# x's normalised combinations made in the first projections, and one PSUM pool for all stages

## The chip, the core and the metric

The kernel runs on one core of a Trainium2 chip. The metric is device time of one execution in microseconds (us), taken as the median of several runs; smaller is better. One execution was also recorded by the hardware profiler, and all rows below come from that one.

## What is computed

One decoder layer on x of 512 tokens by 2048 channels, in fp32. h = RMSNorm(x) goes through one wide projection w_in (2048 rows) that yields the queries, keys and values of three token mixers (A: sliding window, B: forgetting attention, C: cross attention into a memory), a SiLU path z for each of them, and 3 x 2048 columns of merge-gate logits:

```
proj = rms_norm(x, norm_gain) @ w_in
ua = (ya * silu(za)) @ w_branch_a        # ub, uc in the same way
g  = sigmoid(gate_logits).reshape(b, s, 3, D)
y  = g[:, :, 0]*ua + g[:, :, 1]*ub + g[:, :, 2]*uc
out = x + y @ w_out
```

## The kernel before, in words

Every fp32 operand of a matmul is split into a high and a low part (fp32r), and a product is three matmuls: high by high, low by high, high by low. ACT makes the high part (a copy), DVE the low part (a subtraction). 

The program is one order written out by hand: instructions of PE, DVE, ACT and POOL stand in the order in which the Python code emits them. A counter `clock` advances by half a slot for every three matmuls of the main stream (`tick`, line 127), and `later(dt, f)` emits f that many slots afterwards, so that side work is sprinkled between matmuls. The DMAs of SP are not in that order: they are put in order by the building layer, by when their inputs and buffers come free; SP then works through them one after another.

**Main stream** (class `Stream`, line 209). Chunks of up to 512 columns, each of 8 units; a unit takes 2 tiles of 128 rows of w_in and is 24 matmuls. In order: qB0, kB0, vB0 (the first chunk group), qB1, kB1, vB1 (the second), qA0, qA1, kvA, z0, mem, qC, z1, z2, z3. The x operands are the tiles `ah`, `al` (x times norm_gain, high and low; line 63); `rstdb` is the row of 1/rms of all tokens. Unit i asks for the split of unit i+1's weights and for the load of unit i+2's (`run`, line 244): `wa` is the raw tile, `wb` and `wc` the high and low part. A chunk has four PSUM banks from `psum_pj` (tag pj, 4 buffers). The attention heads run beside the stream with banks of the tags T and S (2 buffers each). These 8 banks are one PSUM pool, `ps`.

**z chunks** (`evac_z`, line 909): DVE multiplies each of the four banks by `rstdb` (L926), multiplies the mixer's output y by it (L929), ACT takes the sigmoid, and DVE multiplies again (L932); y then goes to HBM.

**Gates and output** (classes `Late`, `Product`, `Blocks`, lines 1007 to 1212) use a Strassen-Winograd scheme: x is cut into pairs u of two 128-row tiles and two halves of 256 tokens, four blocks a, b, c, d of 128x256; seven products of sums of blocks take the place of eight. A block of gates has 8 units of four products (P1, P5, P6, P4; x operands a, s1, s2, d in `xhx`, `xlx`) and then 8 units of three (P2, P7, P3; operands s3, c, s4 in `yhx`, `ylx`). The banks are tags b0 to b3 with 2 buffers each in a second PSUM pool `pl`, which is opened after `ps` is closed (lines 1470 and 1471).

**The step between them** (`plan_x`, line 1215, and `combine_both`). While z2 and z3 run, each pair u of x is loaded again from HBM (512 KB), DVE normalises it (two 128x512 operations, L1223), makes s1 = b+d, s2 = s1-a, s3 = a-b, s4 = c-s2 (four of 128x256, L1000 and L1003), and the high and low parts are made: 4 blocks into the place of `ah[u]`, `al[u]` as z3 has done with them, 3 blocks into new tiles. `late.step` places the loads, sums and splits of the first gate units in the same stretch.

Of the kernel before, what the change touches and what calls it, by code (L numbers as in the profile page):

```python
# [19 lines left out]
P = 128  # L20
# [23 lines left out]
def tile_hybrid_block(ctx, tc, xT, x, memT, mem, ng, mng, w_in, b_forget, gqa, gka, sinks, gqb, gkb, gqc, gkc,  # L44
# [158 lines left out]

    def psum_pj(name):
        return ps.tile([P, 512], F32, tag="pj", bufs=4, name=name)

    class Stream:
# [37 lines left out]
        def run(self, i):  # L245
# [264 lines left out]
    def tbank(name):  # L510
        return ps.tile([P, 512], F32, tag="T", bufs=2, name=name)

    def sbank(name):
        return ps.tile([P, 512], F32, tag="S", bufs=2, name=name)

    def avbank(name):
        return ps.tile([P, 512], F32, tag="T", bufs=2, name=name)

# [485 lines left out]

    def combine_both(u, xs, s, name, dx):

        bl = blocks(xs)
        a, b, c, d = (bl[:, i, :] for i in range(4))
        add(s[:, 0, :], b, d)
        sub(s[:, 1, :], s[:, 0, :], a)  # L1010
        sub(b, a, b)

        def first():
            h, l = x_tiles(u, name)
            parts(h[:, 0:4:3, :], l[:, 0:4:3, :], bl[:, 0:4:3, :])
            parts(h[:, 1:3, :], l[:, 1:3, :], s, 1)
            later(1, second)

        def second():
            sub(d, c, s[:, 1, :])  # L1020
            parts(*y_tiles(u, name), bl[:, 1:4, :])
        later(dx, first)

# [39 lines left out]
    class Product:  # L1063
# [62 lines left out]
    TAGS = ("b0", "b1", "b2", "b3")  # L1126

# [87 lines left out]
    def plan_x(left):  # L1215


        def one(u, xs, s, free_at):
            fetch_x(xs, u, xT)

            def norm():
                for k in range(2):
                    ve.scalar_tensor_tensor(out=xs[:, k, :], in0=xs[:, k, :], scalar=ngt[:, 2 * u + k:2 * u + k + 1],  # L1223
                                            in1=rstdb, op0=ALU.mult, op1=ALU.mult)
            later(3.5, norm)
            later(4, lambda: combine_both(u, xs, s, "x", max(0.5, free_at - clock[0])))

        def low(u, at):
            t = raw_tile()
            one(u, t[:, 0:2, :], t[:, 2, :].rearrange("p (k n) -> p k n", k=2), at)  # L1230
# [56 lines left out]
    class Branch:  # L1287
# [27 lines left out]
        def run(self):  # L1315
# [87 lines left out]
    def outputs(cpair, tags):  # L1403
# [62 lines left out]
    with tc.tile_pool(name="gp", bufs=1) as pool:  # L1466
        gp.append(pool)
        plan_x(4 * (n_p5 - k))
        run(k, n_p5)
        psp.__exit__(None, None, None)  # L1470
        with tc.tile_pool(name="pl", bufs=2, space=PSUM) as pool:
            gp.append(pool)
            late.run(0, n_gates - 8)
            plan_ys()
            late.run(n_gates - 8, len(late.units))
            flush()
        manual.__exit__(None, None, None)
# [37 lines left out]
```

## Time and profile before

| | us |
|---|---|
| median of 3 runs | 1547.23 (1546.73 to 1547.9) |
| the profiled execution, its own time | 1548.03 |
| its span, first to last instruction | 1546.3 |
| PE busy in the span | 1496.5 (97%) |
| DVE busy | 1085.1 (70%) |
| ACT busy | 723.3 (47%) |
| POOL busy | 269.3 (17%) |

Busy times are sums of instruction times. An engine executes its instructions in order, and one that waits holds back all behind it. PE is the engine that nearly always works, so the places where it does not are where time can go or come from: the view of waits names what ended each of PE's pauses, the timeline shows its instructions one by one (start, duration, and in brackets the pause before it and what ended it), and the windows view gives busy time and the granted clock of TensorE (1.00 is 2.4 GHz, 0.50 is 1.2 GHz) for a stretch. A matmul's row is longer than the step to the next one, since matmuls overlap; what counts is from start to start.

### The profile page before, as it was taken

To read this page: it belongs to the slowest core of one execution; us is meant where nothing else is said; L and a number is where in the kernel's file an instruction comes from. 1 tells how busy PE (TensorE), PEld (TensorE's weight loads), DVE (VectorE), ACT (ScalarE), POOL (GpSimd) and SP (SyncE) were. 2 spreads that over 40 slices of the span, in tenths; PEclk is the share of its full clock that TensorE was granted. 3 is DMA by queue.
4 is the path that set the end of the run, shared out by engine and by line. 5 is a ranking of instruction groups with operands and counts; after the bars stand their busy time and mean duration, and the time that the engine had idled before them with its cause. 6 is when DMAs were issued, how large, how long until landed. Compare 5 with 4: busy or idle time off the path is not lost.

```text
span 1546.3 us, 20410 instructions
## 1 busy us (share of the span) xinstructions
PE 1496.5 (97%) x7233; PEld 1278.0 (83%) x7233; DVE 1085.1 (70%) x1810; ACT 723.3 (47%) x1206; POOL 269.3 (17%) x295
## 2 busy tenths in 40 slices
PE   8999999999999999997999999999999999999998
PEld 7999999998877888875787878787878788877876
DVE  7554664664587755489877777878787656589986
ACT  5434654664477644444435353444445422236432
POOL 3322660661324432100000000000000101110000
PEclk9999999999999999998999999999999999999999
DMA  6443333232254222553667676757676866567583
GB/s 200 135 119 94 89 86 92 76 89 82 89 170 139 81 82 69 163 177 125 229 191 243 192 232 192 235 187 240 194 233 204 286 203 194 171 227 256 191 294 138
DMA packets 118222, 258.53 MB, mean 167 GB/s; under 512 B 13020, under 2 KB 47964, under 8 KB 118120
## 3 DMA queue, kind: packets, MB, share of 16 engines
q1 hardware_dynamic: 113944, 242.54, 49.8%
q10 hardware_dynamic: 4176, 14.69, 2.9%
q8 instruction: 57, 0.93, 0.2%
q14 instruction: 45, 0.37, 0.1%
HBM read 233.04 MB, written 24.14 MB: 166 GB/s over the span
## 4 chain that ended last, share of the span: by engine, by line
PE 71%; DVE 14%; ACT 6%; DMA 4%; issue 3%; SPq 1%; ACTq 0%; POOL 0%; DVEq 0%; POOLq 0%
PE P L1058 27%; PE z L282 8%; PE kB L282 4%; PE vB L282 4%; PE qA L282 4%; PE uB L1058 3%; PE kvA L282 3%; PE uA L1058 3%; PE qC L282 3%; DVE rawl L1003 2%; PE qB L282 2%; DVE R L1000 2%; PE uC L1058 2%; DVE wd L1101 2%; ACT R L1250 2%
## 5 line engine op out<-in xcount | busy, mean ns | idle before, releaser
L1098 ACT CAST wa<-rawl 128x1024 fp32r<-128x1024 f32 x128 | 134.7, 1053 | 257.8 <-PE P L1058 131.0
L196 DVE TENSOR_TENSOR wc<-wa,wb 128x512 fp32r<-128x512 f32 (+2 forms) x254 | 162.1, 667 | 106.4 <-ACT wb L193 105.8
L1003 DVE TENSOR_TENSOR rawl<-rawl 128x512 f32<-128x512 f32 (+1 forms) x265 | 180.6, 682 | 24.8 <-DMA rawl<-in_w_in_dram 14.9
L193 ACT CAST wb<-wa 128x512 fp32r<-128x512 f32 (+2 forms) x254 | 131.3, 565 | 133.1 <-PE z L282 42.2
L1101 DVE TENSOR_TENSOR wc<-rawl,wa 128x1024 fp32r<-128x1024 f32 x128 | 156.3, 1221 | 51.4 <-ACT wa L1098 51.2
L1347 POOL TENSOR_TENSOR y<-y,gA 128x512 f32<-128x512 f32 x16 | 24.7, 1554 | 717.5 <-DMA rawl<-in_w_b_dram 596.9
L1098 ACT CAST wb<-rawl 128x512 fp32r<-128x512 f32 (+1 forms) x128 | 107.1, 837 | 68.9 <-PE P L1058 54.0
L1101 DVE TENSOR_TENSOR wd<-rawl,wb 128x512 fp32r<-128x512 f32 (+1 forms) x128 | 121.8, 951 | 13.8 <-ACT wb L1098 13.7
L282 PE MATMUL z<-ah,wb 128*128 128x512 f32 x256 | 102.5, 400 | 0.8 <-DVE zA L926 0.8
L282 PE MATMUL z<-ah,wc 128*128 128x512 f32 x256 | 100.1, 391 | 0.0
L282 PE MATMUL z<-al,wb 128*128 128x512 f32 x256 | 99.8, 390 | 0.0
L1058 PE MATMUL P<-wa,xhx 128*128 128x512 f32 x192 | 75.8, 395 | 11.2 <-DVE zC L926 11.2
L1058 PE MATMUL P<-wd,xhx 128*128 128x512 f32 x192 | 76.3, 398 | 4.7 <-DVE wd L1101 4.7
L1058 PE MATMUL P<-wb,xhx 128*128 128x512 f32 x192 | 76.0, 396 | 2.0 <-ACT wb L1098 1.3
L1058 PE MATMUL P<-wc,xhx 128*128 128x512 f32 x192 | 75.6, 394 | 0.7 <-DVE wc L1101 0.7
L1058 PE MATMUL P<-wa,xlx 128*128 128x512 f32 x192 | 75.7, 394 | 0.0
L1058 PE MATMUL P<-wb,xlx 128*128 128x512 f32 x192 | 75.0, 390 | 0.0
L1058 PE MATMUL P<-wa,yhx 128*128 128x512 f32 x192 | 74.7, 389 | 0.0
L1058 PE MATMUL P<-wa,ylx 128*128 128x512 f32 x192 | 74.7, 389 | 0.0
L1058 PE MATMUL P<-wc,yhx 128*128 128x512 f32 x192 | 74.7, 389 | 0.0
L1000 DVE TENSOR_TENSOR R<-P,R 128x512 f32<-128x512 f32 x88 | 56.1, 684 | 20.0 <-PE P L1058 19.5
L572 POOL TENSOR_SCALAR pB<-pB,denB 128x128 f32<-128x128 f32 (+3 forms) x48 | 55.3, 1152 | 49.3 <-DVE denB L571 36.5
(385 smaller groups left out, 4022.6 us busy)
## 6 DMA issues: line engine op xcount, KB each, us to landing
rawl<-in_w_in_dram SPq DMA_DIRECT2D x144, 512.0 KB, 4.2
rawl<-in_w_out_dram SPq DMA_DIRECT2D x48, 512.0 KB, 4.6
wa<-in_w_in_dram SPq DMA_DIRECT2D x63, 384.0 KB, 3.3
wa<-in_w_in_dram SPq DMA_DIRECT2D x64, 256.0 KB, 3.0
rawl<-in_w_in_dram SPq DMA_DIRECT2D x48, 256.0 KB, 4.1
gates<-R ACTq DMA_DIRECT2D x24, 512.0 KB, 8.0
wa<-in_w_in_dram SPq DMA_DIRECT2D x16, 512.0 KB, 3.7
wa<-in_w_mem_dram SPq DMA_DIRECT2D x16, 512.0 KB, 3.3
```

Of the source, the lines that this page charges most:

```text
L193: ac.copy(hi[:, :n], raw[:, i, :n])
L196: ve.tensor_sub(lo[:, :n], raw[:, i, :n], f32(hi[:, :n]))
L282: pe.matmul(pb, a, m, start=b in fresh, stop=last and not todo[b])
L572: po.tensor_scalar(p, p, den[:, 4 + i:5 + i], None, op0=ALU.mult)
L1000: ve.tensor_tensor(out, a, b, op=ALU.add)
L1003: ve.tensor_tensor(out, a, b, op=ALU.subtract)
L1058: pe.matmul(*args, **kw)
L1098: ac.copy(hi[:, :k, :], src)
L1101: return lambda: ve.tensor_tensor(lo[:, :k, :], src, f32(hi[:, :k, :]), op=ALU.subtract)
L1250: ac.activation(r, r, AF.Sigmoid)
L1347: po.tensor_tensor(y, y, g, op=ALU.add)
```

## The change

`plan_sums` is new. During the first two chunk groups it loads each pair of x as four pieces of 128x256, normalises them, makes the four sums in place, and stores two sets in HBM: a, s1, s2, d (`x_alpha`, 512 KB a pair) and s3, c, s4 (`x_beta`, 384 KB). The tiles are the places ys3 to ys6, which are empty at that time. `plan_x` then only loads these sets and splits them (one high and one low operation for each set). The loads of the first three gate units are asked for 4 to 6 slots earlier, and for the last z chunk the two y multiplications and the sigmoid are emitted later. There is one PSUM pool of four tags with 2 buffers each for the whole program: T becomes b0, S becomes b1, a chunk's banks 0 and 1 are b2, 2 and 3 are b3. The rotation of tags among gates, branches and outputs is turned by two, so that the first gate products P1, P5, P6, P4 are in b0, b1, b2, b3.

```diff
-    psp = tc.tile_pool(name="ps", bufs=1, space=PSUM)
-    ps = psp.__enter__()
+    ps = ctx.enter_context(tc.tile_pool(name="ps", bufs=2, space=PSUM))
+    TAGS = ("b0", "b1", "b2", "b3")
...
+    xad = nc.dram_tensor("x_alpha", (D // 2, 1024), F32, kind="Internal").ap()
+    xbd = nc.dram_tensor("x_beta", (D // 2, 768), F32, kind="Internal").ap()
...
-    def psum_pj(name):
-        return ps.tile([P, 512], F32, tag="pj", bufs=4, name=name)
+    def bank(i, name):
+        return ps.tile([P, 512], F32, tag=TAGS[i], name=name)
...
-                    banks[b] = psum_pj(f"{name}_{b}")
+                    banks[b] = bank(2 + b // 2, f"{name}_{b}")
...
-            later(0.5, lambda: ve.tensor_tensor(y, y, z, op=ALU.mult))
+            later(1.5 + 1.5 * b if c == 3 else 0.5, lambda: ve.tensor_tensor(y, y, z, op=ALU.mult))
...
-                later(1, lambda: [ac.activation(z, z, AF.Sigmoid) for z, _ in mul])
-                later(4, mul[0][1])
-                later(5, mul[1][1])
+                tail = c == 3
+                later(8 if tail else 1, lambda: [ac.activation(z, z, AF.Sigmoid) for z, _ in mul])
+                later(13 if tail else 4, mul[0][1])
+                later(19 if tail else 5, mul[1][1])
...
-    def combine_both(u, xs, s, name, dx):
...
+    def plan_sums(t0):
+        def one(u, n):
+            xa, xb = (place(i, f"x{i}s{u}").rearrange("p k (t n) -> p (k t) n", t=2) for i in (n, n + 1))
+            a, s1, s2, d = (xa[:, i, :] for i in range(4))
+            s3, c, s4, b = (xb[:, i, :] for i in range(4))
+            rows = [slice((2 * u + k) * P, (2 * u + k + 1) * P) for k in range(2)]
+            halves = [slice(0, 256), slice(256, 512)]
+            for dst, k, h in ((a, 0, 0), (b, 0, 1), (c, 1, 0), (d, 1, 1)):
+                sy.dma_start(out=dst, in_=xT[rows[k], halves[h]])
+            def norm(dst, k, h):
+                ve.scalar_tensor_tensor(out=dst, in0=dst, scalar=ngt[:, 2 * u + k:2 * u + k + 1],
+                                        in1=rstdb[:, halves[h]], op0=ALU.mult, op1=ALU.mult)
+            def store():
+                r = slice(u * P, (u + 1) * P)
+                sy.dma_start(out=xad[r, :].rearrange("p (k n) -> p k n", n=256), in_=xa)
+                sy.dma_start(out=xbd[r, :].rearrange("p (k n) -> p k n", n=256), in_=xb[:, 0:3, :])
+            steps = [lambda: (norm(a, 0, 0), norm(b, 0, 1)), lambda: (norm(c, 1, 0), norm(d, 1, 1)),
+                     lambda: (add(s1, b, d), sub(s2, s1, a)), lambda: (sub(s3, a, b), sub(s4, c, s2)), store]
+            for i, f in enumerate(steps):
+                later(5.5 + 1.5 * i, f)
+        for u in range(NP):
+            at_slot(t0 + (0, 9, 18, 27, 44, 72, 100, 128)[u], lambda u=u: one(u, 3 + 2 * (u % 2)))
...
-                        self.banks[m, t] = gp[1].tile([P, 512], F32, tag=self.tags[n], name=f"{m}_{wcnt[0]}_{t}")
+                        self.banks[m, t] = bank(self.tags[n], f"{m}_{wcnt[0]}_{t}")
...
     def plan_x(left):
-        def one(u, xs, s, free_at):
...
+        def alpha(u):
+            xs = place(2 + u % 2, f"xa{u}").rearrange("p k (t n) -> p (k t) n", t=2)
+            sy.dma_start(out=xs, in_=xad[u * P:(u + 1) * P, :].rearrange("p (k n) -> p k n", n=256))
+            later(5, lambda: parts(*x_tiles(u, "x"), xs, 1))
+        def beta(u):
+            if u % 2 == 0:
+                beta.t = raw_tile()
+            xs = beta.t[:, 2 * (u % 2):2 * (u % 2) + 2, :].rearrange("p k (t n) -> p (k t) n", t=2)[:, 0:3, :]
+            sy.dma_start(out=xs, in_=xbd[u * P:(u + 1) * P, :].rearrange("p (k n) -> p k n", n=256))
+            later(5, lambda: parts(*y_tiles(u, "x"), xs, 1))
         t0 = left - 32
...
+            later(max(0, t0 - 16 + 2.5 * u), lambda u=u: beta(u))
+            later(t0 - 0.5 + 4 * u, lambda u=u: alpha(u))
-        for dt, what, i in ((17, "load", 0), (20, "load", 1), (23, "load", 2), (26, "sums", 0), (28, "early", 0), (29, "sums", 1)):
+        for dt, what, i in ((11, "load", 0), (15, "load", 1), (19, "load", 2), (21, "sums", 0), (23, "sums", 1), (25, "sums", 2),
+                            (28, "early", 0)):
...
-        turn = 2 + 3 * (len(late.units) // (2 * NP))
-        tags = [TAGS[(turn + n) % 4] for n in range(4)]
+        turn = 3 * (len(late.units) // (2 * NP))
+        tags = [(turn + n) % 4 for n in range(4)]
...
     later(20, x_rows)
+    plan_sums(clock[0] + 26)
     run(8, n_p1)
...
-        psp.__exit__(None, None, None)
-        with tc.tile_pool(name="pl", bufs=2, space=PSUM) as pool:
-            gp.append(pool)
```

How the order moves. The rows name line, operation, output<-inputs and shape; a number behind a name tells buffers apart. PE's and POOL's orders stay as they were.

DVE at the end of z3, from the evacuation of its first bank (z_0) to past that of its last (z_3). `wc`, `wd` from a `rawl` are low parts of gate weights, `xlx`, `ylx` low parts of x. Before:

```order
L926 TENSOR_TENSOR zC_7132<-z_0_6780,rstdb 128x512
L1003 TENSOR_TENSOR rawl_7011<-rawl_7011 128x512 x3
L989 TENSOR_TENSOR xlx_7138<-xs_7073,xhx_7137 128x2x256
L926 TENSOR_TENSOR zC_7132<-z_1_6781,rstdb 128x512
L989 TENSOR_TENSOR xlx_7138<-ss_7074,xhx_7137 128x512
L1003 TENSOR_TENSOR xs_7073<-xs_7073,ss_7074 128x256
L929 TENSOR_TENSOR ysC_6212<-ysC_6212,zC_7132 128x1024
L1101 TENSOR_TENSOR wc_7114<-rawl_6979,wa_7113 128x1024
L989 TENSOR_TENSOR ylx_7152<-xs_7073,yhx_7151 128x768
L926 TENSOR_TENSOR zC_7168<-z_2_6782,rstdb 128x512
L926 TENSOR_TENSOR zC_7168<-z_3_6783,rstdb 128x512
L1223 SCALAR_TENSOR_TENSOR xs_7123<-xs_7123,ngt,rstdb 128x512 x2
```

and now:

```order
L992 TENSOR_TENSOR xlx_7186<-xa_7128,xhx_7185 128x1024
L928 TENSOR_TENSOR zC_7231<-z_0_6917,rstdb 128x512
L1112 TENSOR_TENSOR wc_7218<-rawl_7038,wa_7217 128x1024
L992 TENSOR_TENSOR xlx_7226<-xa_7173,xhx_7225 128x1024
L928 TENSOR_TENSOR zC_7231<-z_1_6918,rstdb 128x512
L928 TENSOR_TENSOR zC_7253<-z_2_6919,rstdb 128x512
L1112 TENSOR_TENSOR wd_7240<-rawl_7038,wb_7239 128x1024
L928 TENSOR_TENSOR zC_7253<-z_3_6920,rstdb 128x512
L1112 TENSOR_TENSOR wc_7260<-rawl_7080,wa_7259 128x1024
L931 TENSOR_TENSOR ysC_6340<-ysC_6340,zC_7231 128x1024
```

The norms and sums of the last pairs and the triple weight sums are gone from between the evacuations, and the y multiplication stands behind the second weight part.

DVE in the second and third unit of vB0 (`wc` is a stream weight's low part, `t_kB`, `nr_kB` the norm of the keys). Before:

```order
L401 TENSOR_SCALAR nr_kB_836<-nr_kB_836 128x6
L196 TENSOR_TENSOR wc_859<-wa_798,wb_858 128x384
L407 TENSOR_TENSOR t_kB_808<-t_kB_808,nr_kB_822 128x384
L400 TENSOR_REDUCE nr_kB_850<-sq_kB_856 128x6
L401 TENSOR_SCALAR nr_kB_850<-nr_kB_850 128x6
L196 TENSOR_TENSOR wc_859<-wa_798,wb_858 128x384
L407 TENSOR_TENSOR t_kB_808<-t_kB_808,nr_kB_836 128x384
L407 TENSOR_TENSOR t_kB_808<-t_kB_808,nr_kB_850 128x384
```

and now:

```order
L198 TENSOR_TENSOR wc_867<-wa_804,wb_866 128x384
L1021 SCALAR_TENSOR_TENSOR x4s_782<-x4s_782,ngt,rstdb 128x256
L1021 SCALAR_TENSOR_TENSOR x3s_781<-x3s_781,ngt,rstdb 128x256
L409 TENSOR_TENSOR t_kB_814<-t_kB_814,nr_kB_828 128x384
L402 TENSOR_REDUCE nr_kB_858<-sq_kB_864 128x6
L403 TENSOR_SCALAR nr_kB_858<-nr_kB_858 128x6
L198 TENSOR_TENSOR wc_867<-wa_804,wb_866 128x384
L409 TENSOR_TENSOR t_kB_814<-t_kB_814,nr_kB_842 128x384
L1003 TENSOR_TENSOR x3s_781<-x4s_782,x3s_781 128x256
L1006 TENSOR_TENSOR x3s_781<-x3s_781 128x256
L409 TENSOR_TENSOR t_kB_814<-t_kB_814,nr_kB_858 128x384
```

Two of the four pairs of 128x256 operations on x's first pair (`x3s`, `x4s`) stand among the same rows; the first pair of norms stands a few rows ahead of them, the last two subtractions follow.

SP in vB0 (`wa` are the stream's raw weights, `c_rows` and `cb` belong to attention B). Before:

```order
L183 DMA wa_908<-in_w_in_dram 128x2x384
L183 DMA wa_955<-in_w_in_dram 128x2x384
L183 DMA wa_995<-in_w_in_dram 128x2x384
L183 DMA wa_1040<-in_w_in_dram 128x2x384
L494 DMA c_rows<-f_cum 12x512
L183 DMA wa_1072<-in_w_in_dram 128x2x384
L770 DMA cb_1223<-c_rows 128x512 x2
```

and now:

```order
L185 DMA wa_928<-in_w_in_dram 128x2x384
L1026 DMA x_alpha<-x3s_781 128x1024
L1027 DMA x_beta<-x4s_782 128x768
L185 DMA wa_977<-in_w_in_dram 128x2x384
L1018 DMA x3s_1018<-in_xT_dram 128x256 x2
L1018 DMA x4s_1019<-in_xT_dram 128x256 x2
L185 DMA wa_1029<-in_w_in_dram 128x2x384
L1026 DMA x_alpha<-x5s_905 128x1024
L1027 DMA x_beta<-x6s_906 128x768
L185 DMA wa_1078<-in_w_in_dram 128x2x384
L496 DMA c_rows<-f_cum 12x512
```

The weights' loads have stores of one pair of x and loads of the next but one ahead of them, and a load into `x3s` has to wait until the store from it has landed.

## Rows read from the trace of the kernel before

**Rows 1.** The page, from its first line, part 1 and part 2 (40 equal slices of the span; PEclk is the granted clock in tenths).
```profile
span 1546.3 us, 20410 instructions
...
PE 1496.5 (97%) x7233; PEld 1278.0 (83%) x7233; DVE 1085.1 (70%) x1810; ACT 723.3 (47%) x1206; POOL 269.3 (17%) x295
...
PEclk9999999999999999998999999999999999999999
```

**Rows 2.** The view of waits, engine PE, whole span: who waited for whom, us in total, times, longest.
```profile
PE P L1058 <- DVE zC L926: 11.2, 1, 11.2
```

**Rows 3.** The windows view: stretch, its length, busy time (and instructions) of PE, of PE's weight loads, DVE, ACT, POOL, then granted clock, DMA share, GB/s.
```profile
122.00:249.00 127.00, 126.04 (x761) 123.39 (x760) 73.85 (x185) 71.37 (x160) 61.79 (x80) 1.00 0.32 89
...
642.00:742.00 100.00, 87.21 (x370) 70.43 (x368) 81.27 (x128) 40.42 (x59) 0.00 (x0) 0.93 0.53 173
...
724.00:726.00 2.00, 1.86 (x5) 1.51 (x6) 2.00 (x3) 0.32 (x1) 0.00 (x0) 0.50 0.70 249
...
730.00:735.00 5.00, 5.00 (x24) 4.12 (x23) 4.51 (x7) 1.61 (x3) 0.00 (x0) 1.00 0.34 87
```

**Rows 4.** PE's timeline from the start of z3 to the second gate unit: start, duration, line, what, and in brackets the pause before it and what ended that.
```profile
671.19 0.50 PE L282 MATMUL z<-ah,wb 128*128 128x512 f32 x1 [0.75 <-DVE zA L926]
...
712.59 0.39 PE L282 MATMUL z<-ah,wc 128*128 128x512 f32 x1
724.14 0.77 PE L1058 MATMUL P<-wa,xhx 128*128 128x512 f32 x1 [11.16 <-DVE zC L926]
...
729.25 0.40 PE L1058 MATMUL P<-wb,xhx 128*128 128x512 f32 x1
...
732.24 0.39 PE L1058 MATMUL P<-wa,xlx 128*128 128x512 f32 x1
732.47 0.39 PE L1058 MATMUL P<-wc,xhx 128*128 128x512 f32 x1
...
738.76 0.50 PE L1058 MATMUL P<-wc,xhx 128*128 128x512 f32 x1 [0.70 <-DVE wc L1101]
...
743.09 0.50 PE L1058 MATMUL P<-wd,xhx 128*128 128x512 f32 x1 [1.27 <-DVE wd L1101]
```

**Rows 5.** DVE's timeline around the end of z3, columns as in the group before.
```profile
714.78 0.68 DVE L926 TENSOR_TENSOR zC<-z,rstdb 128x512 f32<-128x512 f32 x1
...
718.03 0.68 DVE L926 TENSOR_TENSOR zC<-z,rstdb 128x512 f32<-128x512 f32 x1
...
720.71 1.22 DVE L1101 TENSOR_TENSOR wc<-rawl,wa 128x1024 fp32r<-128x1024 f32 x1
...
722.71 1.28 DVE L926 TENSOR_TENSOR zC<-z,rstdb 128x512 f32<-128x512 f32 x2
```

**Rows 6.** Groups of DVE instructions by line and shape from 640 to 761 us: count, busy us, mean ns, idle before them.
```profile
L1101 DVE TENSOR_TENSOR wc<-rawl,wa 128x1024 fp32r<-128x1024 f32 x8 | 9.7, 1217 | 0.0
...
L1223 DVE SCALAR_TENSOR_TENSOR xs<-xs,ngt,rstdb 128x512 f32<-128x512 f32 x10 | 7.0, 745 | 0.0
L989 DVE TENSOR_TENSOR ylx<-xs,yhx 128x768 fp32r<-128x768 f32 x5 | 4.8, 955 | 2.7 <-ACT yhx L988 2.7
...
L989 DVE TENSOR_TENSOR xlx<-rawl,xhx 128x512 fp32r<-128x512 f32 x6 | 3.9, 683 | 0.0
L1003 DVE TENSOR_TENSOR rawl<-rawl 128x256 f32<-128x256 f32 x9 | 3.5, 421 | 0.1
```

**Rows 7.** DVE's timeline in vB0 and at the end of vB1.
```profile
90.19 0.56 DVE L196 TENSOR_TENSOR wc<-wa,wb 128x384 fp32r<-128x384 f32 x1 [0.99 <-ACT wb L193]
...
91.80 0.55 DVE L196 TENSOR_TENSOR wc<-wa,wb 128x384 fp32r<-128x384 f32 x1
...
93.57 0.56 DVE L407 TENSOR_TENSOR t_kB<-t_kB,nr_kB 128x384 f32<-128x384 f32 x1 [0.74 <-POOL nr_kB L363]
...
94.31 0.56 DVE L196 TENSOR_TENSOR wc<-wa,wb 128x384 fp32r<-128x384 f32 x1
...
248.81 0.62 DVE L444 SCALAR_TENSOR_TENSOR V_vB<-vB,rstds,V_vB 128x384 fp32r<-128x384 f32 x1 [0.42 <-ACT V_vB L443]
```

**Rows 8.** PE's timeline: the first uses of three of those weight parts, and the first matmul of qA0 into the bank that the last row above sets free.
```profile
93.71 0.33 PE L282 MATMUL vB<-wc,ah 128*128 128x384 f32 x1
...
95.79 0.33 PE L282 MATMUL vB<-wc,ah 128*128 128x384 f32 x1
...
126.42 0.34 PE L282 MATMUL qB<-wc,ah 128*128 128x384 f32 x1
...
249.56 0.36 PE L282 MATMUL qA<-wb,ah 128*128 128x384 f32 x1
```

**Rows 9.** The view of line L196 from 122 to 249 us: duration in ns (least, median, most), first and last start, shape.
```profile
L196 DVE TENSOR_TENSOR wc<-wa,wb x48: 537/555/965, 122.9 to 246.2; 128x384 fp32r<-128x384 f32 x48
```

**Rows 10.** POOL's longest common group by shape from 50 to 340 us: count, busy us, mean ns, idle before.
```profile
L572 POOL TENSOR_SCALAR pB<-pB,denB 128x512 f32<-128x512 f32 x10 | 17.1, 1710 | 17.3 <-DVE denB L571 17.3
```

**Rows 11.** SP's timeline: a run of nine issues of weights; the first, at 115.17, fetches those of the unit that PE starts at 126.16.
```profile
115.17 35.88 SPq L183 DMA_DIRECT2D wa<-in_w_in_dram  x9
```

**Rows 12.** The view of DMA issues: count, KB each, median us from issue to landing.
```profile
wa<-in_w_in_dram SPq DMA_DIRECT2D x63, 384.0 KB, 3.3
...
gates<-R ACTq DMA_DIRECT2D x24, 512.0 KB, 8.0
...
ys_B<-ysB SPq DMA_DIRECT2D x3, 512.0 KB, 4.7
```

More of the change, by code (lines that the diff above doesn't have):

```diff
@@ L510, in tbank @@
     def tbank(name):
-        return ps.tile([P, 512], F32, tag="T", bufs=2, name=name)
+        return bank(0, name)
     def sbank(name):
-        return ps.tile([P, 512], F32, tag="S", bufs=2, name=name)
+        return bank(1, name)
     def avbank(name):
-        return ps.tile([P, 512], F32, tag="T", bufs=2, name=name)
+        return bank(0, name)
     def heads_T(t, col, nt, name):
@@ L1003, in sub @@
         ve.tensor_tensor(out, a, b, op=ALU.subtract)
-    def combine_both(u, xs, s, name, dx):
[L1007 to L1022, printed above, removed]
+    def plan_sums(t0):
[20 more added lines that the diff above has]
+            at_slot(t0 + (0, 9, 18, 27, 44, 72, 100, 128)[u], lambda u=u: one(u, 3 + 2 * (u % 2)))
     class Late:
@@ L1124, in run @@
                         self.done(m, t, o)
-    TAGS = ("b0", "b1", "b2", "b3")
     class Blocks:
@@ L1215, in plan_x @@
     def plan_x(left):
-        def one(u, xs, s, free_at):
[L1219 to L1230, printed above, removed]
@@ L1232, in high @@
-        def high(u, at):
-            n = 2 if u % 2 else 4
-            one(u, place(n, f"xs{u}"), place(n + 1, f"ss{u}")[:, 0, :].rearrange("p (k n) -> p k n", k=2), at)
+        def alpha(u):
[8 more added lines that the diff above has]
+            later(5, lambda: parts(*y_tiles(u, "x"), xs, 1))
@@ L1235, in plan_x @@
         t0 = left - 32
-        freed = [clock[0] + t0 + 4.5 + 4 * u for u in range(NP)]
-        starts = [t0 - 13, t0 - 9, t0 - 5, t0 - 1, t0 + 8, t0 + 20, t0 + 24.5, t0 + 28.5]
         for u in range(NP):
-            later(max(0, starts[u]), lambda u=u: (low if u < 3 else high)(u, freed[u]))
-        for dt, what, i in ((17, "load", 0), (20, "load", 1), (23, "load", 2), (26, "sums", 0), (28, "early", 0), (29, "sums", 1)):
+            later(max(0, t0 - 16 + 2.5 * u), lambda u=u: beta(u))
+            later(t0 - 0.5 + 4 * u, lambda u=u: alpha(u))
@@ L1241, in plan_x @@
+        for dt, what, i in ((11, "load", 0), (15, "load", 1), (19, "load", 2), (21, "sums", 0), (23, "sums", 1), (25, "sums", 2),
+                            (28, "early", 0)):
             later(t0 + dt, lambda what=what, i=i: late.step(what, i))
-        later(left - 1.5, lambda: late.step("split", 0))
+        later(left - 2.5, lambda: late.step("split", 0))
         later(left - 0.5, lambda: late.step("early", 1))
@@ L1319, in run @@
             if first:
-                self.banks["tags"] = tags = TAGS[2 * (ucnt[0] % 2):][:2]
+                self.banks["tags"] = tags = ((2, 3), (0, 1))[ucnt[0] % 2]
                 for b in range(4):
-                    self.banks[b] = gp[1].tile([P, 512], F32, tag=tags[b // 2], name=f"u{br}{self.cg}_{b}")
+                    self.banks[b] = bank(tags[b // 2], f"u{br}{self.cg}_{b}")
                 ucnt[0] += 1
@@ L1367, in pair @@
             for j in range(2):
-                bank = gp[1].tile([P, 512], F32, tag=tags[q if cg < 3 else 1], name=f"yt{u}_{j}")
+                yt = bank(tags[q if cg < 3 else 1], f"yt{u}_{j}")
                 for b in range(4):
-                    pe.transpose(bank[:, b * P:(b + 1) * P], y[b][:, (2 * q + j) * P:(2 * q + j + 1) * P], ident)
-                banks.append(bank)
+                    pe.transpose(yt[:, b * P:(b + 1) * P], y[b][:, (2 * q + j) * P:(2 * q + j + 1) * P], ident)
+                banks.append(yt)
             later(0.5, lambda: out(u, banks))
@@ L1408, in finish @@
             (ac if h else sy).dma_start(out=out[tiles_of(t)[h], cols].rearrange("p (a n) -> p a n", a=2), in_=r)
-        return Blocks(w_out, c, [[TAGS[i] for i in g] for g in tags], finish, resid=x)
-    left = outputs(0, ((3, 0, 1, 2), (0, 1, 2)))
-    right = outputs(1, ((3, 1, 0, 2), (3, 1, 0)))
+        return Blocks(w_out, c, tags, finish, resid=x)
+    left = outputs(0, ((1, 2, 3, 0), (2, 3, 0)))
+    right = outputs(1, ((1, 3, 2, 0), (1, 3, 2)))
     def left_resid(u):
@@ L1469, in tile_hybrid_block @@
         run(k, n_p5)
-        psp.__exit__(None, None, None)
-        with tc.tile_pool(name="pl", bufs=2, space=PSUM) as pool:
-            gp.append(pool)
[L1473 to L1476, printed above, removed]
+        late.run(0, n_gates - 8)
+        plan_ys()
+        late.run(n_gates - 8, len(late.units))
+        flush()
         manual.__exit__(None, None, None)
```

## The prediction, made before the changed kernel ran

> **What bounds the kernel now.** I read the page first. PE is busy 1496.5 of 1546.3 us [rows 1], so only its pauses, some 50 us, and stretches at the lower clock can give time back; what DVE or ACT do counts only where PE waits for it. The page's clock line has one 8 among nines in the middle of the span [rows 1], and the view of waits has one wait that stands out: 11.2 us, once, a gate product for the evacuation of a z bank [rows 2]. Then I read the windows: from 642 to 742 us PE works 87.21 of 100 us at a mean clock of 0.93, DVE works 81.27 and POOL not at all [rows 3]. Last the timelines of PE and DVE there. PE's last z3 matmul starts at 712.59, its first gate matmul at 724.14 [rows 4]. DVE, which has all the sums of x to make in that stretch, evacuates z3's first bank only at 714.78 and the last two from 722.71 to 723.99; the low part of the first gate weights, which the third gate matmul needs, it makes at 720.71 to 721.93 [rows 5]. So two things hold the gates back, 2 us apart: the new PSUM pool needs z3's last evacuation (723.99), and without it PE would still wait for DVE's backlog (721.93).
>
> **What goes away.** In PE's timeline [rows 4]:
> - the pause of 11.16 us before the first gate matmul;
> - the cost of the low clock behind it. The granted clock is 0.50 (1.2 GHz) at 724 to 726 and 1.00 (2.4 GHz) at 730 to 735 [rows 3]. From 724.14 to 729.25 are 12 matmuls in 5.11 us; the next 14, from 729.25 to 732.47, take 0.23 us each, which would be 2.76 for 12: 2.35 us;
> - two waits for the backlog in the second and third gate units, 0.70 and 1.27 us, and 0.75 us at z3's start for z2's last bank, which stood behind norms and sums.
>
> Together 16.23 us. That is all if DVE is no longer late. Its load in the transition: a pair of x costs it two norms (0.745), four 256-wide sums (0.421), two low parts of 512 (0.683) and one of 768 (0.955), 5.5 us [rows 6]; now one low part of 1024 (as the weights' of that shape, 1.217) and one of 768, 2.2 us. For 8 pairs 26.6 us leave a stretch that had 81 busy in 100.
>
> I place the new order's rows behind z3's end, each with its full duration. z3's first bank is done 18 matmuls before the last, 712.59 - 18 x 0.23 + 0.39 = 708.8. Then DVE does z_0 (0.68), the first gate weights' low part (1.22, done 710.7), a low part of x (1.22), z_1, z_2, the second weights' part (done 714.5), z_3 (715.2), the next unit's part (716.4). PE starts the gates at 712.8 and needs these at the third matmul (713.3), for z_0 and z_1 at the 13th (715.6), the second part at the 15th (716.0), z_3 at the 19th (716.9), the next unit at the 25th (718.3). The least margin is 1.5 us. P1 and P5 start in banks b0 and b1, free since the last attention head. So I cost the new transition at zero; its cover is these margins, and what is late next if they go is the second weights' part. The later y multiplications and sigmoids fall in gate units that have room: a unit takes PE 24 x 0.23 = 5.5 us, and DVE two low parts and three 512-wide sums, 4.5 us.
>
> **What is added.** 64 operations of 128x256 on DVE, 8 a pair, in the first two chunk groups. No row has a norm of that shape; it lies between half of the 512-wide norm, 0.37, and all of it, 0.745. I take 0.42, as the sums of the same shape [rows 6]: 3.4 us a pair, 27 us in all, beside matmuls, in a stretch where DVE works 73.85 of 127 us [rows 3]. What reaches PE depends on how late a weights' low part may be. The tightest place is the first pair's, in vB0. There the parts that end at 92.35 and 94.87 [rows 7] are first used at 93.71 and 95.79 [rows 8]: 1.36 and 0.92 us of margin. The order puts two norms ahead of the first half's part at 90.19, covered by a pause of 0.99 before it; two more norms follow (0.84 late at 91.80: covered by 1.36); then two sums, less a pause of 0.74 at 93.57, and two more: 0.84 + 0.84 - 0.74 + 0.84 = 1.8 late against 0.92. That is 0.9 us on PE. The second pair finds it already that late. From the third pair on there are pauses of over 2 us around each place, except the last: two norms ahead of the evacuation at 248.81, which frees a bank for 249.56. It would end at 249.76 and not 249.43, so 0.2 us. Sum 1.1, taken as 1.0; bounds 0, and 6.7 if each pair costs PE 0.84.
>
> POOL shares this stretch: 61.79 us busy of 127, and 0.00 in the transition [rows 3]. The rows say DVE hardly minds: 48 low parts, two inputs from SBUF each, have a median of 0.555 and a most of 0.965 [rows 9], though POOL's commonest long operation takes 1.71 [rows 10]. The Trainium skill (SBUF — State Buffer, Who interferes with whom) says otherwise: a Vector instruction with two SBUF inputs and a GpSimd instruction that reads SBUF exclude each other for the whole of the instruction. All 64 added operations have two such inputs, so by that rule the move goes to the wrong place; the trace agrees only as far as that 0.41 stretch. What full exclusion would cost is a rival below.
>
> SP gets 48 DMAs in these groups, 32 loads and 16 stores, ahead of weights. A weights' load issued at 115.17 [rows 11] is first used at 126.42 [rows 8]; less its landing (3.3 [rows 12]) and about 1 us for its two splits, it may be held 6.9 us. A load of x waits for the store out of its place: 4.7 us as the store of ys_B [rows 12], and four issues of some 0.4: 6.3, hidden. [...] Traffic in the transition grows by 7.3 - 4.2 = 3.1 MB on 17 (173 GB/s for 100 us), with the DMA engines at 0.53 [rows 3]: nothing. PE's and POOL's orders are unchanged; the turned tags cost nothing, since each product has the same two buffers.
>
> **The sum.** 1548.03 (the profiled execution) - 16.23 + 1.0 = 1532.8. The median of the runs is 0.80 lower than that execution, so 1532.0.
>
> **Rivals.**
> - The sums come back in the first groups: DVE is not able to absorb a pair, and each costs PE two operations, 8 x 0.84 = 6.7. For it: margins of 1 us in vB0. Against: DVE idle 42% there. 1531.0 + 6.7 = 1537.7.
> - DVE and POOL exclude each other: the 40 operations in the POOL-busy groups meet POOL at 61.79/127 and wait half of its mean operation (61.79/80 = 0.77): 40 x 0.49 x 0.39 = 7.5, all on PE. Against: the 0.965. 1531.0 + 7.5 = 1538.5. The rule of the Trainium skill's page SBUF — State Buffer, named above, would make it so.
> - The gates still wait: the change does not do what it says, since DVE reaches z_0 as late as now, 714.78 rather than 708.8. 6.0 less the margin of 1.5 is 4.5 us of pause, and 2.4 for the clock: 1532.0 + 6.9 = 1538.9. For it: in-order DVE, with low parts of x that wait for ACT between the evacuations. Against: 26.6 us less work.
> - Slower: SP's queue. If a store in this phase lands as late as the one from ACT's queue, 8.0 [rows 12], and is itself held by the four sums it waits for (1.7), weights behind it are held 8.0 + 1.7 + 1.6 = 11.3, 4.4 beyond the 6.9; six pairs load into places just stored: 26 us, 1558. It decides from a hold of 6.9, and the kernel is slower than before from 6.9 + 16.2/6 = 9.6. Against: the stores of ys_B from SP's queue land in 4.7.
>
> **How the numbers follow.** Forecast 0.65, back in the first groups 0.14, exclusion 0.06, gates still wait 0.08, SP's queue 0.07, of which 0.02 near no change. 1532.0 is the likeliest. The range goes from 1530.0 (no added cost, 1531.0, less the runs' scatter) to 1539.0, which takes in the first four cases. About 0.2%, 3 us, is what a measurement of this kernel can tell from no change; faster 0.92, same 0.03, slower 0.05.
>
> **What would show it.** Right: the first gate matmul within 1 us of the last of z3 and clock 1.00 there; no wait of a gate product for zC; DVE's busy time about the same in all, 27 us more before 250 us and as much less in the transition; PE's wait for `wc` in vB0 under 1.5 us. Wrong: PE waiting for weights (SP), for `wc` at several pairs (DVE), or for `wd` in the first gate units. A gain under 9 us would mean one of the rivals.

## The result, and the profile after

| | before | after |
|---|---|---|
| median, us | 1546.98 (4 runs, 1546.4 to 1547.9) | 1534.53 (4 runs, 1532.27 to 1535.56) |
| the profiled execution, us | 1548.03 | 1534.17 |
| its span, us | 1546.3 | 1532.4 |

The ratio is 0.9919, 95% interval 0.9907 to 0.9932: 0.8% faster, clear of the noise, as forecast, and inside the range; the point, 1532.0, was 2.5 us too low.

The page of after answers to [rows 1]. Its clock line has lost the 8, PE is busy 4 us less, DVE about as much:

```profile
span 1532.4 us, 20507 instructions
...
PE 1492.3 (97%) x7233; PEld 1273.4 (83%) x7233; DVE 1083.6 (71%) x1818; ACT 721.6 (47%) x1198; POOL 272.0 (18%) x295
...
PEclk9999999999999999999999999999999999999999
```

The windows view of after (stretch, length, busy time of PE, PEld, DVE, ACT, POOL, then granted clock, DMA share, GB/s) answers to [rows 3]:

```profile
122.00:249.00 127.00, 124.10 (x746) 120.58 (x745) 81.79 (x209) 69.53 (x157) 64.54 (x80) 1.00 0.43 129
642.00:742.00 100.00, 100.00 (x443) 82.81 (x442) 73.78 (x90) 46.93 (x60) 0.00 (x0) 1.00 0.69 227
724.00:726.00 2.00, 2.00 (x10) 1.67 (x9) 2.00 (x2) 1.55 (x2) 0.00 (x0) 1.00 0.70 260
```

The transition runs without a gap: PE 100.00 of 100 where it was 87.21, at full clock. In the first groups the other side shows, PE down from 126.04 to 124.10 and DVE up from 73.85 to 81.79.

To see where the time went I cut PE's timeline at four matmuls that stand in both programs: the first of kB, of kvA, of z1 and of the first branch product uB. Before:

```profile
50.93 0.34 PE L282 MATMUL kB<-wb,ah 128*128 128x396 f32 x1
...
334.69 0.39 PE L282 MATMUL kvA<-wb,ah 128*128 128x512 f32 x1
...
559.78 0.39 PE L282 MATMUL z<-ah,wb 128*128 128x512 f32 x1
...
1198.07 0.39 PE L1058 MATMUL uB<-wa,ysh 128*128 128x512 f32 x1
```

and after:

```profile
49.23 0.34 PE L284 MATMUL kB<-wb,ah 128*128 128x396 f32 x1
...
337.44 0.39 PE L284 MATMUL kvA<-wb,ah 128*128 128x512 f32 x1
...
562.38 0.39 PE L284 MATMUL z<-ah,wb 128*128 128x512 f32 x1
...
1184.34 0.39 PE L1069 MATMUL uB<-wa,ysh 128*128 128x512 f32 x1
```

| stretch | before | after | change | predicted |
|---|---|---|---|---|
| start to kB | 50.93 | 49.23 | -1.70 | 0 |
| kB to kvA (the sums' new place) | 283.76 | 288.21 | +4.45 | +1.0 |
| kvA to z1 | 225.09 | 224.94 | -0.15 | 0 |
| z1 to uB (the transition) | 638.29 | 621.96 | -16.33 | -16.23 |
| uB to the end | 348.23 | 348.06 | -0.17 | 0 |

The five add up to -13.90, the difference of the spans. The gain has the size that was predicted, by some luck (see the part on the prediction). The cost in the first groups is over four times as large, and 1.7 us of it is hidden in the total by the first 50 us, where PE and DVE do the same work in both programs (last section).

PE's timeline of after shows where most of the 4.45 is lost, the pause and what ended it in brackets:

```profile
95.41 0.44 PE L284 MATMUL vB<-wc,ah 128*128 128x384 f32 x1 [0.76 <-DVE wc L198]
...
123.51 0.45 PE L284 MATMUL qB<-wb,ah 128*128 128x384 f32 x1 [0.41 <-DVE V_vB L446]
...
190.49 0.66 PE L524 MATMUL tkB<-ident,t_kB 128*128 128x128 f32 x4 [0.28 <-DVE plB L551]
221.63 0.44 PE L618 MATMUL ptB<-ident,pB 128*128 128x128 f32 x2 [1.25 <-DVE plB L551]
...
252.17 0.44 PE L284 MATMUL qA<-wb,ah 128*128 128x384 f32 x1
```

Measured as the growth of the lag between the two programs, these five steps are 0.92, 0.56, 0.44, 1.40 and 0.19 us, and a sixth at 87.39 (a kB bank) is 0.24: 3.75 of the 4.45; the rest is in steps under 0.15. DVE's timeline of after has the reason for the first, the second and the fourth of the five:

```profile
94.13 0.42 DVE L1006 TENSOR_TENSOR x4s<-x3s,x4s 128x256 f32<-128x256 f32 x1
94.47 0.42 DVE L1006 TENSOR_TENSOR x4s<-x4s,x3s 128x256 f32<-128x256 f32 x1
94.80 0.55 DVE L198 TENSOR_TENSOR wc<-wa,wb 128x384 fp32r<-128x384 f32 x1
...
122.18 0.42 DVE L1006 TENSOR_TENSOR x6s<-x5s,x6s 128x256 f32<-128x256 f32 x1
122.51 0.42 DVE L1006 TENSOR_TENSOR x6s<-x6s,x5s 128x256 f32<-128x256 f32 x1
122.85 0.61 DVE L446 SCALAR_TENSOR_TENSOR V_vB<-vB,rstds,V_vB 128x384 fp32r<-128x384 f32 x1
...
218.70 0.41 DVE L1003 TENSOR_TENSOR x3s<-x4s,x3s 128x256 f32<-128x256 f32 x1
219.14 0.50 DVE L1006 TENSOR_TENSOR x3s<-x3s 128x256 f32<-128x256 f32 x1
219.57 0.28 DVE L593 CUSTOM_DVE_ANT_0 pB<-sB,biB 128x128 f32<-128x128 f32 x1
...
220.89 0.69 DVE L551 TENSOR_TENSOR plB<-ptB,phB 128x512 fp32r<-128x512 f32 x1 [1.03 <-ACT phB L549]
```

In the first two, two subtractions of a pair of x stand in DVE's order directly ahead of what PE waits for: a weights' low part, and the last evacuation of vB. In the other, four norms and two sums of the seventh pair stand ahead of attention's pB; ACT's phB comes behind pB, DVE's low part plB behind phB, and PE's pause ends 0.05 us after plB. The step at 190.49 is further from its cause: the sixth pair's last operation starts at 180.78, and DVE's first plB behind it (188.43, before 187.24) still has 0.75 us more delay against before than PE has.

At the end of z3 DVE did what was worked out. PE's first gate matmul starts 0.23 us after z3's last, and DVE's evacuations lie where they were placed: z_0 3.9 us before the first gate matmul (predicted 4.0), the second weights' part done 1.4 behind it (1.7), z_3 2.0 behind it (2.4).

```profile
714.00 0.39 PE L284 MATMUL z<-ah,wc 128*128 128x512 f32 x1
714.23 0.39 PE L1069 MATMUL P<-wa,xhx 128*128 128x512 f32 x1
```

```profile
710.35 0.69 DVE L928 TENSOR_TENSOR zC<-z,rstdb 128x512 f32<-128x512 f32 x1 [0.87 <-PE z L284]
710.96 1.22 DVE L1112 TENSOR_TENSOR wc<-rawl,wa 128x1024 fp32r<-128x1024 f32 x1
...
714.42 1.22 DVE L1112 TENSOR_TENSOR wd<-rawl,wb 128x1024 fp32r<-128x1024 f32 x1
715.56 0.69 DVE L928 TENSOR_TENSOR zC<-z,rstdb 128x512 f32<-128x512 f32 x1
```

### The profile page after: what moved, and what is told of

Same layout as the page of the kernel before. It is cut to its first block, busy times and chain, and to the rows that moved or that the text cites. A ratio compares the mean times of both kernels' runs of the same rounds, so it can differ in the third digit from the quotient of the medians.

```text
span 1532.4 us, 20507 instructions
## 1 busy us (share of the span) xinstructions
PE 1492.3 (97%) x7233; PEld 1273.4 (83%) x7233; DVE 1083.6 (71%) x1818; ACT 721.6 (47%) x1198; POOL 272.0 (18%) x295
## 4 chain that ended last, share of the span: by engine, by line
PE 73%; DVE 11%; ACT 6%; DMA 5%; issue 3%; POOL 1%; ACTq 1%; SPq 0%; DVEq 0%; POOLq 0%
PE P L1069 27%; PE z L284 11%; PE uA L1069 4%; PE qA L284 4%; PE kB L284 3%; PE qB L284 3%; PE uB L1069 3%; PE kvA L284 3%; PE uC L1069 3%; DMA rawl<-in_w_in_dram 3%; PE qC L284 3%; PE vB L284 2%; DVE R L1003 2%; DVE rawl L1006 2%; DVE wd L1112 2%
## 5 line engine op out<-in xcount | busy, mean ns | idle before, releaser
L1006 DVE TENSOR_TENSOR rawl<-rawl 128x512 f32<-128x512 f32 x256 | 176.6, 690 | 26.6 <-DMA rawl<-in_w_in_dram 16.5
```

The source lines that it names most:

```text
L1006: ve.tensor_tensor(out, a, b, op=ALU.subtract)
```

## The experiments

Theory A: two things held the gates, the pool and DVE's backlog, and both had to go. Theory B: the cost in the first groups is DVE's order alone. Their rivals are named with each run.

**1. The pool alone.** The change without `plan_sums`; `combine_both`, `plan_x` and the timings of the last z chunk as before.

```diff
-    plan_sums(clock[0] + 26)
```

> The kernel before with one change alone: one PSUM pool of four tags for all stages (turned tags as in the change); x's sums stay in the transition. Theory A (two things held the first gate matmul 2 us apart, the pool's release at 723.99 and DVE's backlog at 721.93): the pause before the first gates shrinks only by about 2 us, to 9, now as a wait for the low part wc of the gate weights, the clock still falls behind it, and the time is about 1545 us (1543.5 to 1546.5). Rival (the pool alone held the gates): pause under 1 us, time about 1531 to 1533.

Measured: 1547.4 (10 runs), before 1547.0, ratio 1.0002 (0.9993 to 1.0011). PE's timeline:

```profile
712.26 0.39 PE L1059 MATMUL P<-wa,xhx 128*128 128x512 f32 x1
712.49 0.39 PE L1059 MATMUL P<-wa,xlx 128*128 128x512 f32 x1
721.46 0.79 PE L1059 MATMUL P<-wc,xhx 128*128 128x512 f32 x1 [8.58 <-DVE wc L1102]
...
738.25 0.50 PE L1059 MATMUL P<-wc,xhx 128*128 128x512 f32 x1 [2.66 <-DVE wc L1102]
```

The wait changed its name and moved by two matmuls, and the clock falls behind it as before (0.50 from 721 to 724). The expected 2 us did not stay: the third unit's pause grew from 0.70 [rows 4] to 2.66 and the second unit got one of 0.69, since DVE still has the same list to work off. From z1 to uB it is 638.36 us, before 638.29.

**2. The sums alone.** The change with the first pool closed and a second opened where the gates begin.

```diff
-        late.run(0, n_gates - 8)
+        psp.__exit__(None, None, None)
+        with tc.tile_pool(name="pl", bufs=2, space=PSUM) as pool:
+            pools.append(pool)
+            late.run(0, n_gates - 8)
```

> The changed kernel, but with two PSUM pools again: the first is closed and a second opened where the gates begin; the sums stay in the first groups. Theory A: the last evacuation of z3 ends at about 716.25 where the first gate matmul now starts at 714.23, so a pause of 2.0 us with z's evacuation as its end, and up to 2.4 us more if the clock falls behind it: 1536.5 to 1539. Rival (moving the sums alone does it): no pause, 1534.5. Other rival (the pool alone did it): a pause near 11 us and 1547 or more.

Measured: 1535.54 (4 runs), ratio to before 0.9928 (0.9915 to 0.9941), a little under the expected 1536.5. The median is 1.0 above that of the change, and the two intervals overlap, so here the trace decides. It has the pause to the hundredth, and no low clock behind it (1.00 from 717 to 725):

```profile
717.44 0.47 PE L1070 MATMUL P<-wa,xhx 128*128 128x512 f32 x1 [2.00 <-DVE zC L929]
```

From z1 to uB: 623.95 us. So of the 16.3 us the sums' move gives 14.3, and the pool the last 2.0 (2.3 counted to the fourth gate unit, see the part on the prediction), which it can give only behind the sums.

**3. Transfers without DVE's work.**

```diff
-                ve.scalar_tensor_tensor(out=dst, in0=dst, scalar=ngt[:, 2 * u + k:2 * u + k + 1],
+                c = slice(256 * h, 256 * h + 16)
+                ve.scalar_tensor_tensor(out=dst[:, 0:16], in0=dst[:, 0:16], scalar=ngt[:, 2 * u + k:2 * u + k + 1],
...
-                     lambda: (add(s1, b, d), sub(s2, s1, a)), lambda: (sub(s3, a, b), sub(s4, c, s2)), store]
+                     store]
```

> The changed kernel with the loads and stores of x's pairs in the first groups kept in number, size and place, but VectorE's part left out: the four norms touch 16 of 256 columns and the four sums are not made (so x's combinations are not computed). From the first kB matmul to the first kvA matmul it was 283.76 us before and 288.21 after, 4.45 more. Theory B (that cost is VectorE's queue: low parts, evacuations and attention's steps that stand behind the inserted operations): 283.8 to 284.7 here, and a time of about 1530.5. Rival (SP's queue and the DMA traffic): still 288, and 1534.5.

The four loads go into the first tile alone here, and the second store comes out of it too, so no store waits for sums. Measured: 284.06 us from kB to kvA, of the 4.45 all but 0.30 is gone; time 1528.17 (4 runs), ratio 0.9876 (0.9863 to 0.9889), 2.3 us less than expected: the profiled execution was also 1.3 us shorter than the change from z1 to uB and 1.3 from uB on, where this edit changes nothing. SP's queue and the traffic cost at most 0.30 in the stretch: from 86 to 122 us the core moved 250 GB/s here, 229 in the change and 119 before, and PE was busy 36.00 of 36, as before.

**4. Twice the sums.**

```diff
-                     lambda: (add(s1, b, d), sub(s2, s1, a)), lambda: (sub(s3, a, b), sub(s4, c, s2)), store]
+                     lambda: [(add(s1, b, d), sub(s2, s1, a)) for _ in range(2)],
+                     lambda: [(sub(s3, a, b), sub(s4, c, s2)) for _ in range(2)], store]
```

> The changed kernel with the four sums of each pair made twice (same values), 32 more operations of 0.42 us on VectorE, 13.4 us, no more transfers. Theory B (VectorE's queue): from the first kB matmul to the first kvA matmul 291 to 294 us where the change has 288.2, time 1537 to 1540. Rival (SP's queue and the DMA traffic): still 288 and 1534.5.

Measured: 297.82 us from kB to kvA in the profiled execution, the slowest of six (1543.83); median 1538.64, ratio 0.9951 (0.9937 to 0.9964). 13.4 us more on DVE cost PE 9.6 there, more than the expected 3 to 6, and the low clock comes with the waits. What it took is, as an estimate from the windows below, 12 x 0.14 + 6 x 0.27 + 6 x 0.28 = 5.0 us of the 9.6. The median, 4.1 us above that of the change, is within what was expected. PE's timeline and the windows:

```profile
97.56 0.44 PE L284 MATMUL vB<-wc,ah 128*128 128x384 f32 x1 [2.31 <-DVE wc L198]
...
128.78 0.68 PE L284 MATMUL qB<-wb,ah 128*128 128x384 f32 x1 [1.08 <-DVE V_vB L446]
```

```profile
98.00:110.00 12.00, 12.00 (x64) 11.85 (x63) 11.36 (x35) 2.58 (x6) 0.00 (x0) 0.86 0.75 243
...
129.00:135.00 6.00, 6.00 (x28) 5.97 (x29) 0.66 (x2) 1.24 (x2) 0.00 (x0) 0.73 0.79 250
230.00:236.00 6.00, 5.61 (x25) 5.42 (x26) 4.64 (x16) 2.93 (x9) 3.03 (x4) 0.72 0.31 122
```

**5. The same operations at other slots.** In the change the four steps of a pair stand at slots 63.5, 65, 66.5, 68 and so on. A unit begins at each multiple of 4 and its two low parts are emitted 0.5 and 1 slot later, so steps at 0, 0.5 and 1 of a unit stand ahead of one or both. Here seven pairs stand at 1.5 or later, and none where a chunk's banks are evacuated. One (107.5 to 112) has steps at 1 and 0 all the same, against what was expected of all; it stands where the change has its fifth pair, and there PE lost at most 0.09 us, so a place ahead of a low part does not always cost:

```diff
+    SLOTS = ((53.5, 55, 57.5, 59), (81.5, 83, 85.5, 87), (97.5, 97.5, 99, 99), (107.5, 109, 110.5, 112),
+             (177.5, 179, 181.5, 183), (185.5, 185.5, 187, 187), (193.5, 193.5, 195, 195), (209.5, 211, 213.5, 215))
+    LOADS = (48, 66, 72, 92, 130, 140, 186, 192)
...
-                later(5.5 + 1.5 * i, f)
+                at_slot(t, f)
```

> The changed kernel with the same 64 operations at other slots: always behind both low parts of a unit and never where a chunk's banks are evacuated; one pair in kB0 (before its end), one late in vB0, two in qB1, none in kB1, two late in vB1, two in qA. Theory B (only the place in VectorE's queue costs): from the first kB matmul to the first kvA matmul 283.8 to 285.2 us where the change has 288.2 and the kernel before 283.8; time about 1530.5 (1528.5 to 1532). Rival (VectorE cannot take a pair in these groups without cost, wherever it stands): 287 to 289 and about 1534.5.

Measured: 283.74 us from kB to kvA, the 283.76 of before; 1529.43 (4 runs, 1528.58 to 1532.31), ratio 0.9894 (0.9878 to 0.9911). The windows of this version: DVE has the work (28.53 of 41 us where before had 22.15), and PE has no gap:

```profile
86.00:122.00 36.00, 36.00 (x211) 35.57 (x210) 23.16 (x59) 13.24 (x29) 9.17 (x12) 1.00 0.57 166
...
208.00:249.00 41.00, 41.00 (x247) 40.43 (x246) 28.53 (x70) 18.73 (x43) 17.39 (x21) 1.00 0.48 149
```

**6. The old timing of z3's multiplications and sigmoids.**

```diff
-            later(1.5 + 1.5 * b if c == 3 else 0.5, lambda: ve.tensor_tensor(y, y, z, op=ALU.mult))
+            later(0.5, lambda: ve.tensor_tensor(y, y, z, op=ALU.mult))
...
-                tail = c == 3
+                tail = False
```

> The changed kernel with the y multiplications and the sigmoids of the last z chunk at their old places, so that two multiplications of 1.2 us stand ahead of the second gate unit's low part on VectorE. By the margins of the changed kernel's trace (second half's part done 715.6, first used at 717.4; the next unit's part done 717.4, first used at 720.4) the 2.3 us are just covered: no wait at the first units, time within 0.5 us of the change, 1534 to 1535.5. Rival (this part of the change is needed): waits of the second and third gate unit for wc or wd of 1 to 3 us, and 1536 to 1538.

Measured: 1533.77 (4 runs), ratio 0.9918 (0.9903 to 0.9933), and one wait of 0.35 us for `wd` in the third unit, where none was expected. From z1 to the fourth gate unit it is 168.86 us, where the change has 168.17: this part of the change is worth 0.7 us there. From z1 to uB the two are equal (621.97 and 621.96), which is chance, as the stretch between scatters by more than that (part on the prediction). In the time it does not show.

**7. The last three pairs alone at the new slots.**

```diff
+    SLOTS = ((63.5, 65, 66.5, 68), (72.5, 74, 75.5, 77), (81.5, 83, 84.5, 86), (90.5, 92, 93.5, 95), (107.5, 109, 110.5, 112),
+             (185.5, 185.5, 187, 187), (193.5, 193.5, 195, 195), (209.5, 211, 213.5, 215))
+    LOADS = (58, 67, 76, 85, 102, 140, 186, 192)
...
-                later(5.5 + 1.5 * i, f)
+                at_slot(t, f)
```

> The changed kernel with the last three pairs alone moved to the places that they have in the spread version (two late in vB1, of which here only the second, and two in qA); the first five stay. By the trace of the change, the stretch from the first kB matmul is longer than before by 2.62 us at the first vB1 matmul and by 4.45 at the first kvA matmul: the first five pairs cost some 2.1 to 2.6, the last three some 2. Theory B (each place pays for itself): 285.7 to 286.4 us from the first kB to the first kvA matmul. Rival (the places hang together: a late VectorE carries on, so that all must move): above 287.

Measured: 285.95 us from kB to kvA, half of the cost, within what was expected; 1529.99 in its one run. As far as one run tells, the places pay separately.

**8 and 9. The change and the version of 5 on one chip**, unaltered, five runs each.

> The changed kernel unaltered, beside the spread version on one chip. 1534.5 us (1533.5 to 1535.5), 288.2 us from the first kB to the first kvA matmul, and 4 to 5 us above the spread version. Rival (the difference between the two was the chips' or the runs'): within 1.5 us of each other.

> The spread version unaltered, on the same chip as the change: 1529.5 us (1528.5 to 1531), 283.8 us from the first kB to the first kvA matmul. Rival: within 1.5 us of the change.

Measured: 1533.79 (1533.62 to 1536.18; ratio to before 0.9924, 0.991 to 0.9937) and 1531.18 (1530.17 to 1533.99; 0.9905, 0.9892 to 0.9918). The difference, 2.6 us, is less than expected. The stretch itself repeats: 288.03 and 283.85 us, 4.2 apart. The spans of the profiled executions are 2.7 apart: the spread version lost 1.72 us before kB (48.74 and 50.46), where the two programs are alike. Between uB and the output products it lost 1.89 more, most of it at a granted clock of 0.83 from 1205 to 1215 us, and had that back by the end (from uB to the end it is 348.93 and 348.65). Experiment 5 against the profile of the change lost 0.78 before kB; that this is chance is likely, but not shown. Of the versions that compute all and ran more than once, that of 5 is the fastest, by 2.6 us on one chip and 5.1 between two.

## Why the prediction was right in what goes, and wrong in what comes

- **The pause and the low clock** (16.23): measured 16.33 from z1 to uB, and no wait of PE between 642 and 742 us. That the two causes lay 2 us apart was read rightly from [rows 4, 5]: the sums alone left a pause of 2.00, and the pool alone left the backlog's wait. The prediction's thought that without the new pool PE would still wait for DVE is experiment 1. Costing the new transition at zero held. The agreement to 0.1 is luck: from z1 to the fourth gate unit (its first matmul starts at 745.53 before and 730.55 after) the gain is 17.58, and in the six further runs with the same transition (experiments 3, 4, 5, 7, 8 and 9) it is 17.57 to 17.65; in experiment 2 it is 15.30. Between that unit and uB 1.25 was lost again, in steps of 0.34 and less, most at the second weights' parts, and there the runs scatter from 452.3 to 453.8 us. The term was 1.35 too small, mostly because the pauses in brackets were added up: a row runs 0.16 beyond the next one's start, so the 11.16 cost 11.32 from start to start, and the first matmul behind a wait is longer (0.50, not 0.39). Both waits for the backlog, 0.70 and 1.27, stand in the third gate unit, not in the second and third.
- **vB0's first pair** (0.9): right for the weights' part, a pause of 0.76 and a step of 0.92. But its first two norms ran at 85.71, ahead of an evacuation of kB, and that step of 0.24 was not in the sum; up to 96 us PE lost 1.43. **The last pair** (0.2): right, 0.19.
- **The step that failed** is the sentence that from the third pair on there are pauses of over 2 us around each place. It sized the added cost at 1.0, and it is 4.45. DVE's pauses were added up over a neighbourhood, but each belongs to a chain of its own. At the seventh pair the trace of before has three, of 0.66, 0.77 and 1.04 us, each ended by another engine (POOL, POOL, ACT):

```profile
214.29 0.56 DVE L407 TENSOR_TENSOR t_kB<-t_kB,nr_kB 128x384 f32<-128x384 f32 x1 [0.66 <-POOL nr_kB L363]
...
216.97 0.29 DVE L591 CUSTOM_DVE_ANT_0 pB<-sB,biB 128x128 f32<-128x128 f32 x1 [0.77 <-POOL biB L601]
...
218.31 0.69 DVE L549 TENSOR_TENSOR plB<-ptB,phB 128x512 fp32r<-128x512 f32 x1 [1.04 <-ACT phB L547]
219.25 0.69 DVE L549 TENSOR_TENSOR plB<-ptB,phB 128x512 fp32r<-128x512 f32 x1
```

 The first pause stands ahead of the pair's norms and is there after, too (0.66). Work that is put in makes pB late, with it ACT's phB and so plB's wait, which stays 1.03 us long (220.89 in after). So neither covers anything, and of the 2.47 us only the 0.77 before pB does. That place alone cost 1.40. The evacuations of vB at the end of vB0, where the fourth pair stands, were not looked at (0.56). The work itself was not underrated: DVE was busy 17.9 us more in the first 250 us (146.81 and 164.69), not 27, since its rows overlap (a norm of 0.48 takes 0.40 from start to start, a subtraction of 0.42 takes 0.34) and the eighth pair came later.
- **The rivals.** "The sums come back in the first groups" came nearest: its mechanism, an ordered queue that makes PE wait, is what happened, at 4.45 of its 6.7, though not at each pair. It was argued against with DVE idle 42% there; the idle share was true and told nothing of the order. SP's queue is refuted by experiments 3 and 5: the 48 transfers stayed, at 0.30 and at no cost. The stores landed in 4.0 and 3.6 us, near the 4.7 that was taken:

```profile
x_alpha<-x3s SPq DMA_DIRECT2D x4, 512.0 KB, 4.0
x_alpha<-x5s SPq DMA_DIRECT2D x4, 512.0 KB, 3.6
```

- **Exclusion of DVE and POOL.** The norms of 128x256 took (least, median, most, in ns):

```profile
L1021 DVE SCALAR_TENSOR_TENSOR x3s<-x3s,ngt,rstdb x8: 466/478/832, 85.7 to 217.7; 128x256 f32<-128x256 f32 x8
...
L1021 DVE SCALAR_TENSOR_TENSOR x6s<-x6s,ngt,rstdb x8: 477/479/480, 97.5 to 252.5; 128x256 f32<-128x256 f32 x8
```

 0.478 against the 0.42 that was taken, and one stretched by 0.35. As a cost of 7.5 to PE the rival did not come: the whole cost is 4.45, and the one stretched norm (0.35, at the seventh pair) replaces a stretch that two weights' parts had there before (1.44 for both at 214.77, elsewhere 1.02). In experiment 5 two norms beside POOL took 0.69 and 0.90, and PE lost nothing. The rule of the Trainium skill (SBUF — State Buffer, Who interferes with whom), that a DVE instruction with two SBUF inputs and a GpSimd instruction that reads SBUF exclude each other for its whole length, would give waits where the two meet. The trace agrees in part: only 8 of the 32 norms meet an instruction of POOL at all, and two of them start inside one POOL instruction (215.17 to 217.13), of which one took 0.83 and the other 0.47. But POOL is slowed as well: its 44 products biB have a median of 0.690 in the change, where it is 0.588 before, 0.592 without DVE's work (experiment 3) and 0.589 in experiment 5, and beside the seventh pair two of them took 0.81 and 1.00 where they took 0.37 and 0.48 before. No pause of PE in the first groups ends with POOL.
- **The total** came nearer than its parts, by luck: 3.45 us too little cost, 0.10 too little gain, and 2.02 us gained in stretches that were costed at zero, 1.70 of them in the first 50 us.

## What to carry to other kernels

Moving work off the place where an engine is late pays what the trace says it pays, if its pauses are counted from start to start. What it costs at the new place depends on what stands right behind each inserted instruction, so look there for the next instruction with a reader that waits (a weights' part, a bank's evacuation, a step of a chain between engines) and at how far lateness carries (10 us at the sixth pair), not at idle shares or pauses added up: the same 64 operations cost 4.45 us at one set of slots and nothing at another. Where two causes hold the same wait, removing the outer one alone gave nothing and the inner one alone all but some 2 us, the distance between them.

## What had not been expected of the hardware

- The start varies more than the rest. In eleven profiled executions, with the same program up to there but for some transfers and the tags of PSUM banks, the first kB matmul came at 48.67 to 50.93 us, and the granted clock from 0 to 50 us was 0.90 to 1.00; experiments 5 and 9, one program, have 1.00 and 0.90. The clock is not all of it: experiment 5 has kB at 50.01 with 1.00, experiment 7 at 48.67 with 1.00.
- Behind a pause of 2.00 us (experiment 2) the granted clock stayed at 1.00, and so it did behind one of 2.41 in the change (1209 us). Behind one of 2.31 (experiment 4) it was 0.86 over the next 12 us, behind one of 2.17 there 0.72 from 230 to 236 us, behind one of 1.82 (experiment 9, 1204.85) 0.83 over 10 us, and behind one of 1.08, which had one of 0.65 shortly before it (126.39 and 128.78), 0.73 over 6 us. The length of the pause alone does not tell; what does, these runs leave open.
